# State-space output products of a two-layer trunk: a contiguous tap table, and state products issued over two tiles and two parities at a time

## The chip, the cores and the metric

The kernel runs on one core of one Trainium2 chip. The metric is the device time of one execution in microseconds. An execution is one launch of the whole trunk.

## The reference, cut to what matters

The reference is a trunk of two layers over 1024 frames of 1024 channels in float32. Layer 0 mixes the frames with an RWKV-7 recurrence. Layer 1 mixes them with a diagonal complex state-space layer. Each mixer is followed by a layer norm, a squared-ReLU MLP of width 4096 and another layer norm. The change touches the state-space layer alone. It has 64 groups of 16 channels, and each group drives 64 complex states:

```python
bu_re = jnp.einsum('tbgc,gpc->tbgp', u_c, bbar_re)
bu_im = jnp.einsum('tbgc,gpc->tbgp', u_c, bbar_im)
pr, pi, sr, si = lax.associative_scan(combine, (a_ch_re, a_ch_im, bu_re, bu_im), axis=0)
carry_re, carry_im = cmul(pr, pi, h_re[None], h_im[None])
s_re = sr + carry_re
s_im = si + carry_im
y = (jnp.einsum('tbgp,gcp->tbgc', s_re, cr_w)
     - jnp.einsum('tbgp,gcp->tbgc', s_im, ci_w))
...
y = y.transpose(2, 0, 1, 3, 4).reshape(bsz, seq, d) + xf * d_skip.astype(f32)
y = jax.nn.gelu(y).astype(x.dtype)
z = y @ w_glu
return z[..., :d] * jax.nn.sigmoid(z[..., d:])
```

## The kernel before

The sequence is worked in two halves of 512 frames, and channels lie on partitions in 8 tiles of 128. Large products (projections, MLP, GLU) take each weight block of 128 x 512 from DRAM (`wload`, L169), split it on ACT and DVE into a high and a low part (`whi` L148, `wlo` L149), and do three matmuls for each 128 x 128 piece (L188). `wraw` has two buffers, `whi` and `wlo` three each. One engine, SP, issues nearly all transfers, in order.

The state-space layer doesn't run frame by frame. It cuts a half into 64 chunks of SL = 8 frames, and it needs three tables, which `s5_tables` builds once, tile by tile (f = 0 to 7, four pairs of groups a tile), and keeps in DRAM:

- `tB` carries a chunk's inputs to its state,
- `tC` carries the state at a chunk's start to the chunk's 8 outputs (the state products),
- `tT` carries the inputs of a chunk to its own outputs (the tap products). It is a banded matrix: the row of input frame s is the same list of taps, shifted by s frames. ACT copies the taps out of PSUM (`pk`) into `kpad`, whose front is zero (L1155), and two transfers a tile read `kpad` with overlapping windows and write the shifted rows to `tT` (L1159). `kpad` is `[128, 16, 16, 4]`, so the four groups g lie innermost, next to each other.

`s5` runs once for each half. It turns the input (`u`, `ug`), makes the chunk states (`pbu`, L1206, into `hb`), runs the scan over chunks on DVE and GpSimd (`advance`), and then makes the outputs in four blocks, f2 = 0 to 3, of two tiles each (j = 0, 1). For each tile it loads `tt` from `tT` (L1240) and `tcm` from `tC` (L1242); both share the tag `tab` with four buffers, so one block fills them all. A parity (par = 0, 1) is one of a pair of groups. For each parity there is one PSUM bank `py` (the pool `pc` has two). Into it go the tap products (L1250: 128 rows of the array, 64 columns, tile j in column half j) and then the state products (L1255: 64 rows, the half named by the parity, and 64 columns, the half named by the tile). ACT copies the bank to `y1` (L1257). TensorE turns it back (`pyt`, L1263), DVE adds the skip term, ACT does the GELU, and SP stores `y` (L1268), which the GLU loads later (`yl`, L946).

The order of the work is set by a scheduler. It takes each step's rank (`rank`: lower comes first, where its inputs are there) and a time that it reckons itself. The state-space layer has rank 99300 or 99400, the tables 99500, and the MLP of the other half comes later by its rank, so MLP matmuls stand in every place between the state-space steps.

Of the kernel before, what the change touches and what calls it, by code (L numbers as in the profile page):

```python
# [8 lines left out]
F32 = mybir.dt.float32  # L9
# [9 lines left out]
HT = 512  # L19
KT = 8  # L20
# [12 lines left out]
TB = 2  # L33
LN8R = 400000
# [36 lines left out]
def trunk(ctx, tc, A):  # L71
    nc = tc.nc
    V, S, G, PE, SP = nc.vector, nc.scalar, nc.gpsimd, nc.tensor, nc.sync
# [88 lines left out]
    def wload(src, kt, n, key=None):  # L162
# [19 lines left out]
        return out  # L182

# [836 lines left out]
    SL = 8  # L1020
    NSC = HT // SL
    tT = dr.tile([KT, 128, 2, 512], F32, name="tT")
# [3 lines left out]
    def s5_tables():  # L1026
# [78 lines left out]
        kpad = pp.tile([128, 16, 16, 4], F32, name="kpad")  # L1105
        G.memset(kpad, 0.0)
        for f in range(KT):
# [45 lines left out]
            for par in range(2):  # L1153
                ps_ = slice(64 * par, 64 * par + 16)
                S.copy(kpad[ps_, 8:].rearrange("p t c g -> p g (t c)"), p[ps_])  # L1155
            tv = tT[f].rearrange("(s c) two n -> two c s n", c=16)
            for par in range(2):
                src = kpad[64 * par : 64 * par + 16, 1:9].rearrange("p t c g -> p (t c g)")
                SP.dma_start(tv[par], bass.AP(src.tensor, src.offset, [src.ap[0], (64, SL), src.ap[1]]))  # L1159
# [13 lines left out]
    def s5(H, h):  # L1173
# [61 lines left out]
        for f2 in range(4):  # L1235
            y1 = s5p.tile([128, SL, 4, 2, 16], F32, tag="u1", name="y1", bufs=2)
            tabs = []
            for f in (2 * f2, 2 * f2 + 1):
                tt = s5p.tile([128, 2, 512], F32, tag="tab", name="tt", bufs=4)
                SP.dma_start(tt, tT[f])  # L1240
                tcm = s5p.tile([128, 4, 2, 128], F32, tag="tab", name="tcm", bufs=4)
                SP.dma_start(tcm, tC[f])  # L1242
                tabs.append((f, tt.rearrange("p two (n g) -> p two g n", g=4), tcm))
            for par in range(2):
                qs = slice(64 * par, 64 * par + 64)
                p = pc.tile([128, HT], F32, tag="c", name="py").rearrange("p (g n) -> p g n", g=4)

                for g2 in range(4):
                    for j, (f, tv, tcm) in enumerate(tabs):
                        PE.matmul(p[64 * j : 64 * j + 64, g2], ug[f][:, 2 * g2 + par], tv[:, par, g2],  # L1250
                                  start=g2 == 0, stop=False, skip_group_check=True)
                for g2 in range(4):
                    for ri in range(2):
                        for j, (f, tv, tcm) in enumerate(tabs):
                            PE.matmul(p[64 * j : 64 * j + 64, g2], hb[qs, 4 * f + g2, ri, 0:NSC], tcm[qs, g2, ri],  # L1255
                                      start=False, stop=ri == 1, skip_group_check=True)
                S.copy(y1[:, :, :, par].rearrange("p t g c -> p g t c"), p.rearrange("p g (t c) -> p g t c", t=SL))  # L1257
# [138 lines left out]
```

## Time and profile before

| | us |
|---|---|
| median of three runs (2736.28 to 2744.62) | 2736.43 |
| the profiled execution | 2746.6 |
| its span in the profile | 2744.8 |
| TensorE busy in the span | 2598.4 |
| tap products, 256 records, first and last start | 1401.4 and 2055.1 |
| state products, 512 records, first and last start | 1481.2 and 2057.1 |

The profile is of one execution on the core, with times from the span's start. Each engine's instructions are grouped by source line and tile names, without buffer numbers. An fp32 matmul of the program is two matmul records in the trace. A record's end is modelled, so records of neighbouring matmuls overlap, and a pace is read from the starts.

### The profile page before, as it was taken

How to read it: one execution, taken by the hardware profiler on the slowest of the kernel's cores; microseconds unless marked ns; L12 is line 12 of the kernel's file. 1: busy time of each engine (PE TensorE's matmuls, PEld its weight loads, DVE VectorE, ACT ScalarE, POOL GpSimd, SP SyncE). 2: the span in 40 equal slices, each digit the busy share in tenths (PEclk: the TensorE clock that was granted, in tenths of full speed). 3: DMA queues.
4: the chain of work that ended last, by engine and by line, in shares of the span. 5: the costliest groups of instructions: out<-in, count | busy, mean ns of one | idle time of the engine just before them, and what ended most of it. 6: DMA issues, size and time to landing. Idle time of an engine off the chain costs nothing.

```text
span 2744.8 us, 43807 instructions
## 1 busy us (share of the span) xinstructions
PE 2598.4 (95%) x16582; PEld 2089.9 (76%) x16582; DVE 1813.3 (66%) x3191; ACT 1154.8 (42%) x2038; POOL 630.6 (23%) x515
## 2 busy tenths in 40 slices
PE   7999979989899999989999999999999999999997
PEld 5778757678677777767876788778778887788886
DVE  7477677577786867997567553674855546755556
ACT  7455574544543333353532332434223324433334
POOL 3121542432442122342122000120220101210101
PEclk9989979999899999999999999999999999999998
DMA  4765455564223334545333533233343322333333
GB/s 146 235 214 175 151 164 156 178 203 142 81 86 88 93 92 148 141 129 163 100 112 127 174 95 100 81 96 112 103 164 110 96 96 81 119 96 96 96 96 100
DMA packets 215058, 345.90 MB, mean 126 GB/s; under 512 B 21184, under 2 KB 75584, under 8 KB 214848
## 3 DMA queue, kind: packets, MB, share of 16 engines
q1 hardware_dynamic: 214848, 343.10, 40.5%
q8 instruction: 131, 2.15, 0.3%
q14 instruction: 79, 0.65, 0.1%
HBM read 279.06 MB, written 63.96 MB: 125 GB/s over the span
## 4 chain that ended last, share of the span: by engine, by line
PE 44%; DVE 4%; issue 3%; DMA 1%; POOL 1%; ACT 1%; ACTq 0%; SPq 0%; DVEq 0%; POOLq 0%
PE d L188 39%; PE py L1250 1%; PE py L1255 1%; DVE wlo L149 1%; DMA wraw<-in_mw_dram 1%; PE pu L154 1%; PE pbu L1206 1%; POOL rl L975 1%; DVE hA L991 0%; DMA s_y<-yg 0%; DVE t L1218 0%; DVE hB L991 0%; ACT whi L148 0%; DVE sq L876 0%; PE pu L1195 0%
## 5 line engine op out<-in xcount | busy, mean ns | idle before, releaser
L148 ACT CAST whi<-wraw 128x512 fp32r<-128x512 f32 x668 | 413.5, 620 | 929.1 <-PE d L188 623.2
L149 DVE TENSOR_TENSOR wlo<-wraw,whi 128x512 fp32r<-128x512 f32 x668 | 500.6, 750 | 426.8 <-ACT whi L148 404.3
L188 PE MATMUL d<-qbuf,whi 128*128 128x512 f32 (+1 forms) x2112 | 657.0, 394 | 23.8 <-DVE hA L991 12.8
L188 PEld LDWEIGHTS d<-qbuf,whi 128*128 128x128 f32 x2112 | 391.8, 191 | 120.0 <-DVE hA L991 17.8
L188 PE MATMUL d<-qbuf,wlo 128*128 128x512 f32 (+1 forms) x1056 | 411.9, 392 | 10.7 <-DVE wlo L149 10.4
L975 POOL TENSOR_TENSOR rl<-rl 128x512 f32<-128x512 f32 x128 | 157.2, 1228 | 1094.5 <-ACT rl L974 1094.5
L188 PE MATMUL d<-oAh,whi 128*128 128x512 f32 (+1 forms) x960 | 390.9, 411 | 15.5 <-ACT ev L418 6.3
L188 PE MATMUL d<-oAl,whi 128*128 128x512 f32 (+1 forms) x960 | 387.5, 405 | 3.0 <-DVE oAl L149 2.8
L188 PE MATMUL d<-oAh,wlo 128*128 128x512 f32 (+1 forms) x960 | 386.5, 405 | 2.4 <-DVE wlo L149 2.3
L188 PE MATMUL d<-oBh,whi 128*128 128x512 f32 x704 | 279.2, 397 | 0.0
L188 PE MATMUL d<-oBh,wlo 128*128 128x512 f32 x704 | 278.7, 396 | 0.2 <-DVE wlo L149 0.2
L188 PE MATMUL d<-oBl,whi 128*128 128x512 f32 x704 | 277.1, 394 | 0.0
L188 PEld LDWEIGHTS d<-qbuf,wlo 128*128 128x128 f32 x1056 | 201.7, 191 | 56.5 <-DVE wlo L149 14.5
L188 PEld LDWEIGHTS d<-oAh,whi 128*128 128x128 f32 (+1 forms) x960 | 185.9, 194 | 62.2 <-ACT ev L418 8.4
L188 PEld LDWEIGHTS d<-oAh,wlo 128*128 128x128 f32 (+1 forms) x960 | 185.8, 194 | 44.4 <-DVE wlo L149 3.2
L188 PEld LDWEIGHTS d<-oAl,whi 128*128 128x128 f32 (+1 forms) x960 | 185.6, 194 | 43.1 <-DVE oAl L149 5.2
L991 DVE TENSOR_TENSOR hB<-hB,d 128x512 f32<-128x512 f32 (+1 forms) x256 | 165.0, 650 | 71.2 <-PE d L188 68.0
L991 DVE TENSOR_TENSOR hA<-hA,d 128x512 f32<-128x512 f32 x240 | 162.1, 682 | 64.4 <-PE d L188 62.1
L188 PEld LDWEIGHTS d<-oBh,wlo 128*128 128x128 f32 x704 | 132.9, 189 | 32.4 <-issue 2.0
L188 PEld LDWEIGHTS d<-oBl,whi 128*128 128x128 f32 x704 | 133.1, 189 | 29.9 <-issue 0.7
L188 PEld LDWEIGHTS d<-oBh,whi 128*128 128x128 f32 x704 | 133.1, 189 | 29.0 <-issue 1.2
L149 DVE TENSOR_TENSOR qbuf<-rl,qbuf 128x512 fp32r<-128x512 f32 x128 | 95.0, 742 | 73.5 <-ACT qbuf L148 73.5
(374 smaller groups left out, 3804.8 us busy)
## 6 DMA issues: line engine op xcount, KB each, us to landing
wraw<-in_mw_dram SPq DMA_DIRECT2D x520, 256.0 KB, 2.7
wraw<-in_glu_dram SPq DMA_DIRECT2D x64, 256.0 KB, 2.7
low<-wlo SPq DMA_DIRECT2D x52, 256.0 KB, 2.6
wlo<-low SPq DMA_DIRECT2D x52, 256.0 KB, 3.6
wraw<-in_wk_dram SPq DMA_DIRECT2D x32, 256.0 KB, 3.5
wraw<-in_wr_dram SPq DMA_DIRECT2D x32, 256.0 KB, 3.9
wraw<-in_wv_dram SPq DMA_DIRECT2D x32, 256.0 KB, 4.3
yl<-s_y SPq DMA_DIRECT2D x32, 256.0 KB, 3.1
```

The source lines that it names most:

```text
L148: S.copy(hi, src)
L149: (e or V).tensor_sub(lo, src, hi.bitcast(F32))
L154: PE.matmul(out, x, idt, start=True, stop=True)
L188: bulk.append((PE.matmul(p, w, x, **kw).ins, x.shape[-1]))
L975: G.tensor_mul(r, r, r)
L991: V.tensor_add(z, z, p)
L1206: PE.matmul(p[qs, g2, ri], tb[:, g2, ri, qs], u[:, 2 * g2 + par], start=True, stop=True)
L1250: PE.matmul(p[64 * j : 64 * j + 64, g2], ug[f][:, 2 * g2 + par], tv[:, par, g2], start=g2 == 0, stop=False, skip_group_check=True)
L1255: PE.matmul(p[64 * j : 64 * j + 64, g2], hb[qs, 4 * f + g2, ri, 0:NSC], tcm[qs, g2, ri], start=False, stop=ri == 1, skip_group_check=True)
```

## The change

There are two edits and one helper.

The tap table `tT` becomes one array with the partition first, `[128, 2, KT, 4, 128]`, in which the 128 taps of a group lie next to each other; `kpad` is laid out the same way and holds TBF = 4 tiles. ACT's copies fill it tile by tile. After every fourth tile, 16 transfers (two parities by eight shifts) write four tiles at once, in runs of 512 bytes; before, two transfers a tile wrote runs of 2 KB. The load of a tile takes two runs of 2 KB a partition instead of one of 4 KB, and the tap matmuls read their 128 columns with unit stride instead of a stride of four.

The output block takes both `py` banks at its start, does the tap products of both parities, and then the state products with the loops turned: pair of groups, real and imaginary, tile, parity. `inorder` ties each state product to the one before it by a dependence without a semaphore, so the scheduler keeps them in this order. Both banks are copied out at the end.

```diff
+    def inorder(prods):
+        for x, y in zip(prods, prods[1:]):
+            tc.add_manual_dep(y.ins, x.ins.name, mybir.DependencyInfo(
+                mybir.DependencyClass.NoSync, mybir.DependencyReason.DATA), reason="order")
...
-    tT = dr.tile([KT, 128, 2, 512], F32, name="tT")
+    tT = dr.tile([128, 2, KT, 4, 128], F32, name="tT")
...
-        kpad = pp.tile([128, 16, 16, 4], F32, name="kpad")
+        kpad = pp.tile([128, TBF, 4, 16, 16], F32, name="kpad")
...
-                S.copy(kpad[ps_, 8:].rearrange("p t c g -> p g (t c)"), p[ps_])
-            tv = tT[f].rearrange("(s c) two n -> two c s n", c=16)
-            for par in range(2):
-                src = kpad[64 * par : 64 * par + 16, 1:9].rearrange("p t c g -> p (t c g)")
-                SP.dma_start(tv[par], bass.AP(src.tensor, src.offset, [src.ap[0], (64, SL), src.ap[1]]))
+                S.copy(kpad[ps_, f % TBF, :, 8:].rearrange("p g t c -> p g (t c)"), p[ps_])
+            if f % TBF == TBF - 1:
+                for par in range(2):
+                    for s in range(SL):
+                        SP.dma_start(
+                            tT[16 * s : 16 * s + 16, par, f - TBF + 1 : f + 1].rearrange("c f g n -> c (f g) n"),
+                            kpad[64 * par : 64 * par + 16, :, :, 1 + s : 9 + s].rearrange("c f g t e -> c (f g) (t e)"))
...
-                SP.dma_start(tt, tT[f])
+                SP.dma_start(tt.rearrange("p two (g n) -> p two g n", g=4), tT[:, :, f])
...
-                tabs.append((f, tt.rearrange("p two (n g) -> p two g n", g=4), tcm))
+                tabs.append((f, tt.rearrange("p two (g n) -> p two g n", g=4), tcm))
+            pp = [r.tile([128, HT], F32, tag=t, name="py").rearrange("p (g n) -> p g n", g=4)
+                  for r, t in ((pc, "c"), (pc, "c"))]
+            for g2 in range(4):
+                for par in range(2):
+                    for j, (f, tv, tcm) in enumerate(tabs):
+                        PE.matmul(pp[par][64 * j : 64 * j + 64, g2], ug[f][:, 2 * g2 + par], tv[:, par, g2],
+                                  start=g2 == 0, stop=False, skip_group_check=True)
+            prods = []
+            for g2 in range(4):
+                for ri in range(2):
+                    for j, (f, tv, tcm) in enumerate(tabs):
+                        for par in range(2):
+                            qs = slice(64 * par, 64 * par + 64)
+                            prods.append(PE.matmul(pp[par][64 * j : 64 * j + 64, g2], hb[qs, 4 * f + g2, ri, 0:NSC],
+                                                   tcm[qs, g2, ri], start=False, stop=ri == 1, skip_group_check=True))
+            inorder(prods)
             for par in range(2):
-                qs = slice(64 * par, 64 * par + 64)
-                p = pc.tile([128, HT], F32, tag="c", name="py").rearrange("p (g n) -> p g n", g=4)
-                for g2 in range(4):
-                    for j, (f, tv, tcm) in enumerate(tabs):
-                        PE.matmul(p[64 * j : 64 * j + 64, g2], ug[f][:, 2 * g2 + par], tv[:, par, g2],
-                                  start=g2 == 0, stop=False, skip_group_check=True)
-                for g2 in range(4):
-                    for ri in range(2):
-                        for j, (f, tv, tcm) in enumerate(tabs):
-                            PE.matmul(p[64 * j : 64 * j + 64, g2], hb[qs, 4 * f + g2, ri, 0:NSC], tcm[qs, g2, ri],
-                                      start=False, stop=ri == 1, skip_group_check=True)
-                S.copy(y1[:, :, :, par].rearrange("p t g c -> p g t c"), p.rearrange("p g (t c) -> p g t c", t=SL))
+                S.copy(y1[:, :, :, par].rearrange("p t g c -> p g t c"), pp[par].rearrange("p g (t c) -> p g t c", t=SL))
```

What the scheduler makes of it shows in the order of each engine's instructions (line numbers of the changed kernel are higher by 7 to 15). First TensorE in the first half's third output block, before:

```order
L1250 MATMUL py<-tt,ug 64x128
L1263 MATMUL pyt<-ident,y_13970 128x64 x16
L1250 MATMUL py<-tt,ug 64x128 x7
L1255 MATMUL py<-tcm,hb 64x128
L1250 MATMUL py<-tt,ug 64x128 x5
L1255 MATMUL py<-tcm,hb 64x128 x15
L1250 MATMUL py<-tt,ug 64x128 x3
L1255 MATMUL py<-tcm,hb 64x128 x16
```

and the same block in the changed kernel, with the next MLP matmul (L195) behind it:

```order
L1260 MATMUL py<-tt,ug 64x128
L1278 MATMUL pyt<-ident,y_13986 128x64 x16
L1260 MATMUL py<-tt,ug 64x128 x15
L1268 MATMUL py<-tcm,hb 64x128 x32
L195 MATMUL d<-oBh,wlo 128x512
```

All tap products now stand ahead of all state products; before, the kinds took turns. Inside such a block, with buffer numbers, the place where tap products (from `tt`) give way to state products (from `tcm`) in the second block of the changed kernel; py_13995 and py_13996 are the banks of the two parities, tcm_13989 and tcm_13993 the tables of the two tiles:

```order
L1260 MATMUL py_13995<-tt_13991,ug_13597 64x128
L1260 MATMUL py_13996<-tt_13987,ug_13566 64x128
L1260 MATMUL py_13996<-tt_13991,ug_13597 64x128
L1268 MATMUL py_13995<-tcm_13989,hb_13451 64x128
L1268 MATMUL py_13996<-tcm_13989,hb_13451 64x128
L1268 MATMUL py_13995<-tcm_13993,hb_13451 64x128
L1268 MATMUL py_13996<-tcm_13993,hb_13451 64x128
```

Four state products in a row name the four pairs of tile and parity, and the next four do so again. Before, 16 of one parity stood in a row, with the tile changing from one to the next.

Second, SP while the tables are built, before (two `tT` stores a tile):

```order
L1144 DMA tC<-ca 1024x1x128
L169 DMA wraw<-in_wo_dram 128x512 x2
L1159 DMA tT<-kpad 16x8x512 x2
L169 DMA wraw<-in_wo_dram 128x512
L1110 DMA bc<-in_s5bc_dram 128x256
```

and in the changed kernel around the first row of `tT` stores:

```order
L170 DMA wraw<-in_mw_dram 128x512
L1166 DMA tT<-kpad 16x16x128 x16
L1177 DMA tB<-bs 128x1024
L1151 DMA tC<-ca 1024x1x128
L1117 DMA bc<-in_s5bc_dram 128x256
L170 DMA wraw<-in_mw_dram 128x512 x4
```

The stores stand in two rows of 16 instead of eight pairs, and weight loads wait behind each row.

More of the change, by code (lines that the diff above doesn't have):

```diff
@@ L33 @@
 TB = 2
+TBF = 4
 LN8R = 400000
```

## The prediction

> **What bounds the kernel now.** I read the page first, for the busiest engine:
>
> ```profile
> PE 2598.4 (95%) x16582; PEld 2089.9 (76%) x16582; DVE 1813.3 (66%) x3191; ACT 1154.8 (42%) x2038; POOL 630.6 (23%) x515
> ```
>
> A share over the whole span says little about one stage, so the second view is busy time by stretches (start and end, length, then busy time and instructions of PE, PE's weight loads, DVE, ACT and POOL, the granted clock, DMA's share and GB/s). 1480 to 1535 and 2008 to 2062 are the output products of the two halves of the state-space layer, where the change's matmuls run; 1180 to 1240 is the worst part of the table building.
>
> ```profile
> 1480.00:1535.00 55.00, 55.00 (x503) 41.16 (x502) 22.63 (x30) 18.75 (x31) 8.68 (x5) 0.98 0.63 221
> 2008.00:2062.00 54.00, 54.00 (x489) 40.33 (x489) 22.00 (x29) 17.66 (x31) 9.49 (x6) 0.97 0.56 195
> ...
> 1180.00:1240.00 60.00, 49.40 (x239) 37.46 (x237) 56.91 (x81) 30.89 (x50) 26.36 (x19) 0.86 0.43 113
> ```
>
> In both output stages TensorE is busy all of the time, DVE and ACT under half. What those products take is paid in the end time, since mlp matmuls fill every space between them and would simply come earlier. In the table stage it is the other way: DVE is at 57 of 60 and PE has 10 us of holes.
>
> Third, PE in order of time through three of the four output blocks of the first half (start, length, line, operation, count). Each fp32 matmul of the program stands as two records.
>
> ```profile
> 1381.98 2.09 PE L1206 MATMUL pbu<-ug,tb 128*64 128x64 f32 x64
> ...
> 1401.39 1.07 PE L1250 MATMUL py<-tt,ug 128*64 128x128 f32 x4
> 1407.86 3.84 PE L1250 MATMUL py<-tt,ug 128*64 128x128 f32 x28
> ...
> 1481.22 3.55 PE L1255 MATMUL py<-tcm,hb 64*64 64x128 f32 x64
> ...
> 1489.03 0.65 PE L1250 MATMUL py<-tt,ug 128*64 128x128 f32 x2
> 1489.60 1.01 PE L1263 MATMUL pyt<-ident,y 64*128 64x64 f32 x16
> 1490.55 2.01 PE L1250 MATMUL py<-tt,ug 128*64 128x128 f32 x14
> 1492.49 1.96 PE L1255 MATMUL py<-tcm,hb 64*64 64x128 f32 x32
> 1494.38 2.01 PE L1250 MATMUL py<-tt,ug 128*64 128x128 f32 x16
> 1496.33 1.96 PE L1255 MATMUL py<-tcm,hb 64*64 64x128 f32 x32
> ...
> 1503.26 0.65 PE L1250 MATMUL py<-tt,ug 128*64 128x128 f32 x2
> ...
> 1504.78 2.01 PE L1250 MATMUL py<-tt,ug 128*64 128x128 f32 x14
> 1506.71 0.43 PE L1255 MATMUL py<-tcm,hb 64*64 64x128 f32 x2
> 1507.07 1.56 PE L1250 MATMUL py<-tt,ug 128*64 128x128 f32 x10
> 1508.56 1.96 PE L1255 MATMUL py<-tcm,hb 64*64 64x128 f32 x30
> 1510.45 1.10 PE L1250 MATMUL py<-tt,ug 128*64 128x128 f32 x6
> 1511.48 1.96 PE L1255 MATMUL py<-tcm,hb 64*64 64x128 f32 x32
> ```
>
> A row's length holds its last record's tail, 0.07 of which lies beside the next row (2.01 against 1492.49 - 1490.55 = 1.94). Two paces come out, with the length of one record from this view:
>
> ```profile
> L1255 PE MATMUL py<-tcm,hb x512: 269/269/473, 1481.2 to 2057.2; 64*64 64x128 f32 x171
> L1250 PE MATMUL py<-tt,ug x256: 388/406/422, 1401.4 to 2055.1; 128*64 128x128 f32 x128
> ```
>
> State products (L1255): the two tiles of a block sit in two column halves and start together, so 32 records are 16 starts; (1.96 - 0.27) / 15 = 0.113 us a step. Tap products (L1250): 16 records are 8 starts, (2.01 - 0.41) / 7 = 0.229, for the same 128 columns. The tap table is read with a stride of four elements ("n g" rearranged), the state table is not. Full height isn't the reason: L1206 also uses 128 rows by 64 columns, reads unit stride, and puts 64 records of half the width into 2.09. With 0.22 off for its last record, an estimate from its shorter streaming, that is 0.060 a step, 0.12 for 128 columns.
>
> **The change part by part.** First, the tap products read contiguously. I take 0.113 for the step, as in L1255; the ends are 0.229 (nothing gained, if the layout is not what slows them) and 0.113. By the changed order a block has one tap matmul ahead of the transposes and 15 behind, and the two kinds no longer alternate. Now the lone one takes 0.57 to the next row, and a run of 7 steps 1.94, of which 0.34 is its end. Then the lone one is 0.57 - 2 x 0.116 = 0.35, the other 15 are 15 steps of 0.113 and an end of 0.34 - 0.12 = 0.22, so 1.92: 2.27 a block. The first block of a half (2 matmuls, then 14) gets 0.56 + 1.92. Per half 0.56 + 1.92 + 3 x 2.27 = 9.3. Before, tails taken off: 1.00 + 3.77 in the first block, 0.57 + 1.94 + 1.95 in the second, 0.57 + 1.93 + 1.49 + 1.03 = 5.02 in the third and, by its like order, the fourth: 19.3. Saved 10.0 a half, **20.0 in all** (the second stage is as full and as long).
>
> Second, the state products, four in a row: tile and parity change from one to the next, over two banks, so all four quarters of the array are named in turn. Before, one parity's 16 stood whole before the other's. Whether four quarters run at once, the trace shows in one place: in the first block the parities follow each other without anything between (the x64 row), and there the number of records in flight, in windows of 10 ns, goes up:
>
> ```profile
> 1482.50:1482.51 0.01, 0.01 (x6) 1.00 0.53 205
> 1482.98:1482.99 0.01, 0.01 (x8) 1.00 0.00 0
> 1483.09:1483.10 0.01, 0.01 (x10) 1.00 0.00 0
> 1483.70:1483.71 0.01, 0.01 (x4) 1.00 0.00 0
> ```
>
> A record lasts 0.27, so two a step of 0.11 keep 5 in flight and four keep 10. At the seam it is 10: four quarters at the pair's own step. I take that: 15 x 0.113 + 0.19 (1.89 less 15 steps) = 1.89 a block, and 0.2 more in the first, whose start is slow: 7.8 a half. Before: 3.48 + (1.89 + 1.89) + 2 x (0.36 + 1.89 + 1.89) = 15.5. Saved 7.7 a half, **15.5 in all**; the other end is 0 (pairs only).
>
> The Trainium skill speaks against this: "TensorE: Matmul & The Clock Gate", section "Part 3: Packing small matmuls — row/col tiling", has matmuls start and end strictly in program order. The seam differs: in strict order five records of the first parity and the second's first pair, some seven, could be in flight there, not ten. By the rule the 15.5 would be 0; the measurement decides, and the first rival is worked out below.
>
> Third, what is put at risk in the output stage. Its transfers stay and their time shrinks. SP's issues there, and what moved from 1488 to 1534 with the median time to landing:
>
> ```profile
> 1497.27 0.42 SPq L1268 DMA_DIRECT2D s_y<-yg  x1
> 1498.32 0.32 SPq L1240 DMA_DIRECT2D tt<-tT  x1
> 1498.73 0.46 SPq L1242 DMA_DIRECT2D tcm<-tC  x1
> ...
> DMA packets 4123, 10.86 MB, mean 236 GB/s; under 512 B 458, under 2 KB 458, under 8 KB 4120
> ...
> tt<-tT SPq DMA_DIRECT2D x4, 512.0 KB, 5.1
> ```
>
> The second tile's tables can be asked for only when the block before has let go of their buffers (1496.33 + 1.89 = 1498.22, and tt goes out at 1498.32), and SP, in order, also holds a store and a load of y ahead of them. Should those make tt 1.0 late, it lands 6.1 behind the state products; the next block's second tile wants it after the mlp matmuls (1498.22 to 1503.26, 5.0), one tap (0.35) and the transposes (1490.55 - 1489.60 = 0.95), 6.3 behind. It just fits, and any delay on SP becomes a wait of the tap matmuls, with all of PE behind them. A block to block time of 14.2 (1489.03 to 1503.26) becomes 10, and the 10.86 MB of 46 us have to pass in about 32, 340 GB/s. I charge 5 us in all (six seams of just under 1 us), from 0 to 14.
>
> Fourth, the tables. Rows of the building:
>
> ```profile
> L1155 ACT COPY kpad<-pk x16: 1055/1074/1087, 1126.9 to 1267.7; 16x512 f32<-16x512 f32 x16
> L1159 SPq DMA_DIRECT2D tT<-kpad x16: 320/362/1264, 1128.6 to 1268.9; - x16
> 1072.42 0.96 POOL L1106 MEMSET kpad<- 128x1024 f32 x1 [0.91 <-POOL rl L975]
> 1075.99 1.11 POOL L975 TENSOR_TENSOR rl<-rl 128x512 f32<-128x512 f32 x1 [2.61 <-ACT rl L974]
> ACT whi L148 <- DMA wraw<-in_mw_dram: 23.0, 12, 3.9
> ```
>
> The memset, four times as long at 3.9 us, ends 0.3 after POOL's next square could start: nothing. The 16 copies on ACT write contiguously and may halve (0.5 us each, on an engine at half load): nothing. Eight pairs of stores become two rows of sixteen, 16 x 0.36 = 5.8 us each on SP, with a table store and the weight loads behind them; ACT already waits 23 us there for late weights. Against that, six of eight places where SP stands still for a copy go. The next copy into the same slot comes about 20 us later (eight pairs in 141 us) and the row is through in 5.8 + 5, so that wait hides. I charge 1 us, from -5 to +8.
>
> Sum: -20.0 - 15.5 + 5 + 1 = -29.5 on the profiled 2746.6, 2717.1. That execution stands 0.37% over the median of 2736.43, so 2717.1 x 0.9963 = 2707.
>
> **The rivals.** A: PE starts matmuls only in order. The two records of a matmul need the same quarter, so each matmul's second record holds the next matmul back: eight records take four steps, the pair's rate. The taps alone, with less haste in the transfers: -20.0 + 2 + 1 = -17, 2719. For it: the only four-wide stretch is a few steps long, and no run of any length here issues four quarters. It is the page's rule above. B: transfers set the pace of the output stage. If it gets no more than the 269 GB/s of one 20 us stretch there, 10.86 MB take 40 us instead of 32: 16 in place of the 5, -18.5, 2718; at today's 236 GB/s -6.5, 2730. Rows for B and for C:
>
> ```profile
> 1500.00:1520.00 20.00, 10.03 (x100) 6.56 (x102) 0.00 (x0) 1.17 (x2) 1.00 0.74 269
> ...
> 545.01 1.71 PE L596 MATMUL pA<-AR,KB 64*128 64x128 f32 x16
> ```
>
> DMA is at 0.74 there, so full use would be about 360, above what is needed. C, slower: changing the row half at each matmul empties the array. A lone state matmul (the x2 row) takes 0.36 to the next row; at that price the 256 of them take 92 us instead of 31: -20 + 61 + 3 = +44, 2780. It decides from (31 + 20) / 256 = 0.20 us a matmul. Against it: pA changes row halves at each matmul, and (1.71 - 0.27) / 15 = 0.096 a record shows no emptying (no overlap either, which leans to A, though its weights are twice as wide).
>
> **How the numbers follow.** Forecast 0.68, A 0.13, B 0.12, C 0.03, unforeseen stalls from the reordering 0.04. The range runs from 35.5 saved with 5 gained in the tables (-40.5, 2696) up to 2722, past A and B's nearer end; B's far end, C and both costs at their worst stay out. A measurement here tells 0.3%, 8.2 us. Faster: the forecast, A and most of B, 0.90; same 0.05; slower 0.05.
>
> **What would show it.** Tap steps of 0.11 instead of 0.23; 64 state records in about 1.9 with ten in flight; PE full from block to block. Wrong: tap steps still near 0.23 (layout no cause); state runs of 3.5 (A); PE waiting ahead of tap matmuls for tt (B); holes of several us behind the rows of sixteen stores.

## The result, and the profile after

The changed kernel takes 2754.73 us (median of four runs, 2754.32 to 2756.34), against 2738.43 for the kernel before on the same chip (four runs, 2736.28 to 2744.62). The ratio is 1.0057, with a 95% interval from 1.0044 to 1.0070: slower by 15.6 us, where 29.5 less were forecast. The profiled execution took 2754.32, its span 2752.5. Since the profiled execution of before was one of its longer ones, the two spans differ by 7.7 only. The engines over the span:

```profile
PE 2572.3 (93%) x16582; PEld 2078.3 (76%) x16582; DVE 1814.6 (66%) x3191; ACT 1145.8 (42%) x2038; POOL 631.8 (23%) x515
```

TensorE is busy 26.1 us less than before (2598.4), but the part of the span in which it stands still went from 146.4 (2744.8 - 2598.4) to 180.2. The products did get cheaper. TensorE in the changed kernel's second block of outputs, in order of time (start, length, line, count):

```profile
1508.21 1.01 PE L1278 MATMUL pyt<-ident,y 64*128 64x64 f32 x16
1509.16 1.96 PE L1260 MATMUL py<-tt,ug 128*64 128x128 f32 x30
1511.05 1.98 PE L1268 MATMUL py<-tcm,hb 64*64 64x128 f32 x64
```

Here 30 records of tap products stand for 15 matmuls. They take 1.89 (1511.05 - 1509.16), 0.126 a step with the run's end in it, where a step took 0.229 before. The 64 state records take 1.91 to the next row (1512.96), 30 ns a record. So both products run as forecast where nothing disturbs them. Where the time went shows in TensorE's busy time by stretches (stretch, length, busy time, granted clock, DMA's share, GB/s), first before:

```profile
1100.00:1350.00 250.00, 230.97 (x1253) 0.96 0.49 136
...
1470.00:1550.00 80.00, 76.13 (x583) 0.96 0.56 191
...
1990.00:2080.00 90.00, 85.84 (x625) 0.96 0.45 153
```

and then the changed kernel:

```profile
1100.00:1350.00 250.00, 213.25 (x1081) 0.90 0.46 125
...
1470.00:1550.00 80.00, 68.43 (x599) 0.91 0.55 177
...
1990.00:2080.00 90.00, 76.54 (x632) 0.92 0.46 148
```

In the table stage (1100 to 1350) and in the two output stages TensorE lost 17.7, 7.7 and 9.3 us of busy time, and in each the granted clock of what was left is lower by 0.04 to 0.06. In each stretch between these (0 to 1100, 1350 to 1470, 1550 to 1990, 2080 to 2700) the two kernels differ by 1.4 us of busy time or less.

In the table stage, SP shows why:

```profile
1167.12 0.33 SPq L170 DMA_DIRECT2D wraw<-in_mw_dram  x1
1167.49 19.48 SPq L1166 DMA_DIRECT2D tT<-kpad  x16
...
1191.15 1.80 SPq L170 DMA_DIRECT2D wraw<-in_mw_dram  x2
```

The row of sixteen stores holds SP for 19.48 us, 1.2 a store and not 0.36, and the next weights are asked for 24 us after the last. The second row does the same:

```profile
1271.41 19.16 SPq L1166 DMA_DIRECT2D tT<-kpad  x16
1290.67 1.12 SPq L1177 DMA_DIRECT2D tB<-bs  x1
1291.88 2.49 SPq L170 DMA_DIRECT2D wraw<-in_mw_dram  x2
```

The waits between 1165 and 1300 (engine, line, releaser: us in total, times, longest) carry it on to TensorE:

```profile
ACT whi L149 <- DMA wraw<-in_mw_dram: 31.7, 5, 20.4
...
PE d L195 <- ACT whi L149: 16.1, 2, 13.5
...
ACT kpad L1162 <- DMA tB<-bs: 7.1, 1, 7.1
PE pb L1175 <- ACT kpad L1162: 6.9, 1, 6.9
```

The waits of 20.4 and 13.5 belong to the second row. Before, ACT's longest wait for weights was 3.9. Behind the first row TensorE stood still twice, for 6.9 us and, from 1193.62, for another 2.6, until a copy of weights that ACT began at 1195.54. The 6.9 come from `kpad` itself: ACT's next copy into it waits for all stores of the row, and it starts at 1191.87, when the last of them has landed (1191.70; the view names `tB`, whose store lands later, at 1192.94). Without that wait TensorE would still have lacked weights until 1196.2, so both holes together, some 9.5 us, are what the late weights alone would have cost there. In the output stage, SP's order stands in front of the second tile's tables:

```profile
1526.25 0.33 SPq L1283 DMA_DIRECT2D s_y<-yg  x1
1526.67 0.52 SPq L1249 DMA_DIRECT2D tt<-tT  x1
1527.29 1.51 SPq L1251 DMA_DIRECT2D tcm<-tC  x1
1529.88 0.32 SPq L953 DMA_DIRECT2D yl<-s_y  x1
1531.94 0.32 SPq L1283 DMA_DIRECT2D s_y<-yg  x1
1532.36 0.52 SPq L1249 DMA_DIRECT2D tt<-tT  x1
```

The first tile's tt is asked for at 1526.67, the second's at 1532.36, behind a load of y that waits for its store and a store that waits for its GELU. TensorE wants the second at 1534 and gets it at 1538.36 (in brackets the wait ahead of the row):

```profile
1521.60 3.51 PE L1260 MATMUL py<-tt,ug 128*64 128x128 f32 x30 [2.01 <-DMA tt<-tT]
...
1538.36 3.67 PE L1260 MATMUL py<-tt,ug 128*64 128x128 f32 x30 [4.42 <-DMA tt<-tT]
```

The same 30 records that took 1.96 above now take 3.51 and 3.67. The stretches of these two rows say why; the granted clock is the number behind the brackets:

```profile
1521.60:1525.00 3.40, 3.40 (x30) 3.11 (x30) 1.84 (x3) 1.66 (x3) 0.87 (x1) 0.53 0.55 152
...
1538.40:1542.00 3.60, 3.60 (x34) 3.27 (x34) 2.09 (x3) 1.15 (x2) 0.00 (x0) 0.50 0.34 123
```

So these waits of 2.0 and 4.4 us cost their own length and some 1.7 us more, because the clock stands at half for the next 3.5 us. Not every such wait does that: in the third and eighteenth run below, waits of 2.20 and 2.42 us ahead of the same records left the clock at 1.00 and the records at 1.96.

### The profile page after: what moved, and what is told of

The parts are those of the page before. It is cut to its first block, busy times and chain, and to the rows that moved or that the text cites. A ratio compares the mean times of both kernels' runs of the same rounds, so it can differ in the third digit from the quotient of the medians.

```text
span 2752.5 us, 43811 instructions
## 1 busy us (share of the span) xinstructions
PE 2572.3 (93%) x16582; PEld 2078.3 (76%) x16582; DVE 1814.6 (66%) x3191; ACT 1145.8 (42%) x2038; POOL 631.8 (23%) x515
## 4 chain that ended last, share of the span: by engine, by line
PE 58%; DVE 15%; DMA 5%; issue 4%; ACT 3%; SPq 2%; POOL 1%; ACTq 0%; DVEq 0%; POOLq 0%
PE d L195 51%; DVE wlo L150 3%; SPq L1166 1%; DMA yl<-s_y 1%; DMA s_y<-yg 1%; PE pA L603 1%; DVE hA L998 1%; DMA wraw<-in_mw_dram 1%; DMA ldsg<-s_sg 1%; PE pu L155 1%; PE pbu L1215 1%; DVE t L1227 1%; DVE hB L998 1%; DVE xh L648 1%; DVE x L646 1%
## 5 line engine op out<-in xcount | busy, mean ns | idle before, releaser
L195 PE MATMUL d<-qbuf,whi 128*128 128x512 f32 (+1 forms) x2112 | 659.3, 395 | 40.0 <-DVE hA L998 14.2
L195 PEld LDWEIGHTS d<-qbuf,whi 128*128 128x128 f32 x2112 | 393.7, 192 | 136.2 <-DVE hA L998 20.6
L195 PE MATMUL d<-qbuf,wlo 128*128 128x512 f32 (+1 forms) x1056 | 412.8, 393 | 9.2 <-DVE wlo L150 8.8
L195 PE MATMUL d<-oAh,whi 128*128 128x512 f32 (+1 forms) x960 | 390.0, 410 | 16.3 <-ACT ev L425 5.2
L195 PE MATMUL d<-oAl,whi 128*128 128x512 f32 (+1 forms) x960 | 386.8, 404 | 2.5 <-DVE oAl L150 2.2
L195 PE MATMUL d<-oAh,wlo 128*128 128x512 f32 (+1 forms) x960 | 385.9, 405 | 2.5 <-DVE wlo L150 2.0
L195 PE MATMUL d<-oBh,whi 128*128 128x512 f32 x704 | 278.5, 396 | 0.7 <-ACT whi L149 0.7
L195 PE MATMUL d<-oBh,wlo 128*128 128x512 f32 x704 | 278.1, 395 | 0.0
L195 PE MATMUL d<-oBl,whi 128*128 128x512 f32 x704 | 277.5, 394 | 0.0
L195 PEld LDWEIGHTS d<-qbuf,wlo 128*128 128x128 f32 x1056 | 201.9, 191 | 56.2 <-DVE wlo L150 14.1
L195 PEld LDWEIGHTS d<-oAh,whi 128*128 128x128 f32 (+1 forms) x960 | 185.2, 194 | 61.3 <-ACT ev L425 7.3
L195 PEld LDWEIGHTS d<-oAh,wlo 128*128 128x128 f32 (+1 forms) x960 | 185.3, 193 | 44.8 <-DVE wlo L150 3.4
L195 PEld LDWEIGHTS d<-oAl,whi 128*128 128x128 f32 (+1 forms) x960 | 185.4, 193 | 42.6 <-DVE oAl L150 4.7
L195 PEld LDWEIGHTS d<-oBh,wlo 128*128 128x128 f32 x704 | 132.8, 189 | 32.2 <-issue 2.0
L195 PEld LDWEIGHTS d<-oBl,whi 128*128 128x128 f32 x704 | 132.8, 189 | 30.2 <-issue 1.3
L195 PEld LDWEIGHTS d<-oBh,whi 128*128 128x128 f32 x704 | 133.0, 189 | 29.0 <-ACT whi L149 1.3
```

The lines of the kernel that those rows point to most:

```text
L195: bulk.append((PE.matmul(p, w, x, **kw).ins, x.shape[-1]))
```

## The experiments

Each kernel ran beside the kernel before on the same chip; ratios are to that kernel, with 95% intervals. A difference between two ratios is turned into us with 2738; with intervals of some 0.001 to 0.002 to either side, such a difference is good to 5 to 8 us. "Output stages" below means, for each half, from the first state product to the last transpose: 52.7 us twice before, with TensorE busy throughout, 50.5 and 46.6 in the changed kernel with 42.4 and 40.2 busy. Some 496 records of TensorE run in it in every kernel, or 502 in the first half of those with the long rows of stores.

### Which of the two parts

**First run**: the kernel before, with the changed output block (both banks, products four in a row) and the old table.

```diff
 kernel before
+            prods.append(PE.matmul(pp[par][...], hb[...], tcm[qs, g2, ri], ...))
+            inorder(prods)
```

> The old table (strided, two stores a tile) with the new order of the state products alone. Theory T: both products got cheaper as forecast (some 35 us), and holes on TensorE with a lower granted clock behind them took it back, some 25 us in the table stage (two rows of sixteen stores) and some 25 in the two output stages (waits for tt). Here the table stage is that of before, so T expects no holes there, state products at 1.9 us a block, -15.5 from these, and some of it lost at the seams, since a block still keeps its long taps (4 us): 0 to 8. So 7 to 15 us less than before. Rival R1 (the rows of stores are the whole loss): -15 to -16. Rival R2 (the output stage loses whatever is gained there, since its transfers set the pace): 0, within 3 us of before. Rival R3 (the four-in-a-row order itself costs time outside, by the clock): slower than before.

Measured: 0.9997 [0.9981, 1.0013], about 1 us less. The 31.2 us of state products before (from each start to the next, waits taken out, over all 512 records) became 15.3. The stages shrank to 46.0 and 46.6, so 12.8 us are there to be seen, but TensorE waits 2.7 and 3.2 in them. T's 7 to 15 isn't met, nor R1's 15 to 16, and R2's number is. Where the rest of the 12.8 went this run doesn't say; the fourteenth comes back to it.

**Second run**: the changed kernel with the old output block.

```diff
 changed kernel
-            inorder(prods)
+            for par in range(2): ... taps, then states of one parity
```

> The contiguous table with its two rows of sixteen stores, and the state products in the old order, one parity after the other. T: tap products -20, table stage +25, seams of the output stage 5 to 12: between 10 and 17 us slower than before, so about the changed kernel's time or a little more (the state products bring nothing, and less is lost at the seams). R1: +5 (-20 + 25). R2: +25, since the taps bring nothing and the table stage loses what it lost. R3: faster than before, by some 10 to 20 us.

Measured: 1.0059 [1.0039, 1.0080], 16 us slower. The tap products went from 38.6 to 21.4, and the table stage lost as much as in the changed kernel (77.9 of 100 busy from 1200 to 1300, at a clock of 0.84). That is T's case; the numbers of R1, R2 and R3 aren't met.

### The table stage

**Third run**: the contiguous table, stored tile by tile.

```diff
-    tT = dr.tile([128, 2, KT, 4, 128], F32, name="tT")
+    tT = dr.tile([KT, 128, 2, 4, 128], F32, name="tT")
...
-            if f % TBF == TBF - 1:
-                ... 16 stores of [16, 16, 128], four tiles at once
+            for par in range(2):
+                for g in range(4):
+                    SP.dma_start(tv[par, :, :, g], ...)   # [16, 8, 128], one tile
```

> The changed kernel, but the table is stored tile by tile, eight stores of 64 KB a tile (a parity and a pair of groups each, runs of 512 bytes as before), instead of two rows of sixteen of 128 KB. The same bytes, twice the stores, no row in front of the weight loads longer than eight. T: the two holes of the table stage (13.5 and 6.9 us, and the clock behind them) shrink to a third or less: 15 to 25 us less than the changed kernel, 0 to 10 less than before. R1: 25 to 50 us less than the changed kernel, since all loss was there. If the number of 512-byte packets costs, however they are dealt out, the 64 stores take SP as long in all, and the gain is under 8 us. R3: no change against the changed kernel.

Measured: 0.9975 [0.9961, 0.9988], 7 us less than before and 22 less than the changed kernel. TensorE in the table stage:

```profile
1100.00:1350.00 250.00, 228.78 (x1269) 0.98 0.48 136
```

That is near before (230.97) again, with the same packets of 512 bytes and twice the stores. The output stages are much as in the changed kernel (48.7 and 48.5, with 39.3 and 40.9 busy). So the bunching of the stores costs, not the layout of the taps, and some 23 us of the forecast are still missing. The order of the tiles in DRAM changes with this edit too; the fifteenth run below keeps the changed kernel's and shows the same.

**Eighth run**: the long rows, issued by GpSimd.

```diff
-                        SP.dma_start(tT[16 * s : 16 * s + 16, ...], kpad[...])
+                        G.dma_start(tT[16 * s : 16 * s + 16, ...], kpad[...])
```

> The changed kernel with its two rows of sixteen stores of the table, but issued by GpSimd in place of SP. The packets and bytes are the same, in the same two bursts. If the holes of 6.9 and 13.5 us come from SP, which stands 19 us in a row and can't issue the weight loads behind it (T): the holes go, and 15 to 25 us less than the changed kernel. If they come from the DMA engines, busy with 2048 packets of 512 bytes a burst, so that weights would be late whoever issues (R4): the holes stay at half their size or more, and under 10 us gained.

Measured: 1.0072 [1.0059, 1.0085], nothing gained. (A row is 4096 packets of 512 bytes, 2.1 MB, not the 2048 of the expectation.) SP is free now and asks for the weights, but they are late all the same. The DMA issues from 1172 to 1216 (count, KB each, median us from issue to landing):

```profile
tT<-kpad POOLq DMA_DIRECT2D x16, 128.0 KB, 9.7
wraw<-in_mw_dram SPq DMA_DIRECT2D x7, 256.0 KB, 8.7
```

and the same weights among the pairs of stores of before (1125 to 1190):

```profile
wraw<-in_mw_dram SPq DMA_DIRECT2D x6, 256.0 KB, 3.0
```

So R4 holds in this form: the burst fills the DMA engines, and SP's queue only shows it. GpSimd's queue cut the stores into packets of other sizes and held up GpSimd's own work, so how much of the loss comes from which isn't told apart here. The rate of such a burst can be read from both kernels, before (one pair, 0.5 MB):

```profile
1128.60:1133.60 5.00, 5.00 (x26) 4.13 (x25) 4.81 (x6) 2.29 (x5) 3.56 (x3) 1.00 0.79 148
```

and after (one row, 2.1 MB):

```profile
1167.50:1190.00 22.50, 16.08 (x91) 11.07 (x90) 18.62 (x29) 4.25 (x8) 6.10 (x4) 1.00 0.75 111
```

At a DMA share of 0.75 to 0.79 these stores out of 16 partitions move 111 to 148 GB/s; in an output stage a share of 0.72 moves 247 (fourteenth run, quoted below). The bytes take the engines about as long in eight pairs as in two rows: eight times under 5 us, hidden behind the weights in hand, or twice 19.

**Fifteenth run**: rows of half the size.

```diff
-TBF = 4
+TBF = 2
```

> The changed kernel with TBF = 2: four rows of sixteen stores, each store 64 KB, in place of two rows with 128 KB. The same bytes and packets, the same layout. A row holds 1 MB, which at the 110 GB/s of the long rows takes the DMA engines some 9 us instead of 19. Theory T on the table stage (the weights in hand cover some 7 to 10 us; what a burst lasts longer is a hole): the holes of 6.9 and 13.5 us shrink to 0 to 3 each, and 12 to 22 us less than the changed kernel. If a hole's size goes with the bytes stored and not with the burst's length: no change.

Measured: 1.0010 [0.9998, 1.0022], 13 us less than the changed kernel. The first and the last of the four rows on SP:

```profile
1142.31 9.42 SPq L1166 DMA_DIRECT2D tT<-kpad  x16
...
1263.84 9.68 SPq L1166 DMA_DIRECT2D tT<-kpad  x16
```

With a row's length the time goes: eights that hold SP about 4 us 0.9975, rows of 9.6 us 1.0010, rows of 19.3 us 1.0057. The holes are smaller (3.4, 2.7, 3.3 and 2.0 us, and one of 4.2 ahead of a pk), but not gone. A row of 9.6 leaves a hole of some 3. One of 19.2 left 13.5, and one of 19.5 left 9.5 (6.9 and 2.6). So the weights in hand cover some 6 to 10 us, near the 7 to 10 that I had put into T.

### The output stages: a wait that is handed on

**Fourth run**: yg in slots that are free by then.

```diff
-                y = s5p.tile([128, HT], F32, tag="yg", name="yg", bufs=1)
+                y = s5p.tile([128, HT], F32, tag="ug", name="yg", bufs=8)
```

> The changed kernel, but yg (the result that is stored to y) takes the slots of ug that the block's taps have set free, instead of one buffer of its own, so DVE and ACT no longer wait for a store to land before they turn to the next tile. The transfers stay, with both stores of a block ahead of the second tile's tables. If the single buffer is what makes tt late (theory T1 on the seams): the waits for tt shrink to a third, and 10 to 20 us less than the changed kernel. If tt is late because SP asks for it only when a block's last state product has read the buffers, and the table then takes 5 to 6 us to land (T2): under 5 us less, and the waits for tt stay. R1: no change, since the seams cost nothing.

Measured: 1.0064 [1.0044, 1.0084], no gain. The waits ahead of the taps stayed (1.9 and 2.9 in the first half, 4.6 and 0.8 in the second). T1 falls.

**Fifth run**: the third run's kernel, y stored by ACT.

```diff
-                SP.dma_start(scr["y"][...], y)
+                S.dma_start(scr["y"][...], y)
```

> The kernel of the third run (four-in-a-row products, contiguous table stored in eights) with one more edit: ACT issues the stores of y, behind its own GELU, in place of SP, so the loads of the next tables on SP no longer stand behind a store that waits for DVE and ACT. Theory T3 (SP's order: the second tile's tt is asked for some 4 us after its buffer is free, because the store ahead of it waits for its GELU): the waits for tt, some 13 us in two stages, go to under 4, and 8 to 20 us less than the third run's kernel, so 14 to 26 less than before. Rival B (the transfers set the pace; DMA's share in the stage is 0.73 over 42 us): the waits stay, moved by a microsecond or two, and under 4 us gained. Rival T2 (the buffers come free too late, after the last state product, and a table needs 5 us): the waits shrink by a quarter at most, under 5 us.

Measured: 1.0030 [1.0017, 1.0043], 15 us slower than the third run, against every theory's number. SP's waits in the first output stage (1470 to 1560), in the third run:

```profile
SPq L1283 <- ACT yg L1282: 16.5, 7, 6.5
SPq L953 <- DMA s_y<-yg: 14.0, 8, 3.7
```

and in the fifth:

```profile
SPq L953 <- DMA s_y<-yg: 40.1, 8, 8.2
```

The wait for the GELU left SP, but what SP has next, the load of y, waits for the same store to land, and with a single yg these loads go out 7 to 10 us apart. The tables still stand behind it. T3 named the right queue and the wrong instruction.

**Sixth run**: the fifth with yg in the slots of ug (the fourth run's edit). **Seventh run**: the sixth with a block's loads as tt, tt, tcm, tcm.

```diff
+                SP.dma_start(tt, ...)    # both tiles first
+                SP.dma_start(tcm, ...)
```

> The kernel of the fifth run, and yg in the slots of ug that the taps have set free (as in the fourth run). T3: the stores no longer stand in front of the tables, so the single buffer could only delay DVE and ACT; with it gone too, 0 to 6 us less than the fifth run. If the single buffer was what held the blocks back all the time, only masked in the fourth run by SP's order: 8 to 15 us less than the fifth run. B: no change.

> The kernel of the sixth run, with the loads of a block in the order tt, tt, tcm, tcm in place of tt, tcm, tt, tcm, so both tap tables take the buffers that the taps set free, some 2 us ahead of those that the state products set free. T2: 5 to 12 us less than the sixth run. T3 or B: within 4 us of it.

Measured: 0.9981 [0.9969, 0.9993] and 0.9982 [0.9971, 0.9993]. The sixth is 13 us below the fifth, as the theory of a masked buffer had it, and no better than the third. The seventh gains nothing: its waits for tt are gone, and waits for tcm stand in their place (5.2 and 4.5 us in the two stages). So T2's number isn't met; but SP still stood with the loads of y, so this run alone doesn't exclude T2. The thirteenth does: its buffers come free no sooner, and the waits are nearly gone. SP in the sixth run (1470 to 1560):

```profile
SPq L953 <- DMA s_y<-yg: 16.3, 5, 6.3
```

**Ninth run**: the sixth with the loads of y by GpSimd. **Tenth run**: the ninth with the taps of one parity alone loaded (and used for both). **Twelfth run**: the same edits on y, with the old table.

```diff
-            SP.dma_start(y, scr["y"][k * 128 : ...])
+            G.dma_start(y, scr["y"][k * 128 : ...])
...
-                SP.dma_start(tt, ...)                      # tenth run
+                SP.dma_start(tt[:, 0], tT[f, :, 0] ...)
```

> The kernel of the sixth run, with the loads of y for the GLU (yl) issued by GpSimd. SP now issues only tables and weights in the output stage; in the sixth run it stood 16.3 and 14.7 us in the two stages with a yl that waited for its store to land, the next tt behind it. T3 (SP's order is what makes tt late): waits ahead of tap products from 6 to 8 us a stage to under 2, and 10 to 20 us less than the sixth run, so 15 to 25 us less than before. T2 or B (buffers come free too late for a load of 5 us, or the transfers set the pace): 0 to 5 us less than the sixth run, and the waits stay at 5 us or more a stage.

> The kernel of the ninth run, but only the taps of one parity are loaded, and both parities' products use them: a quarter of the tables' bytes is left out, and the output isn't the reference's. TensorE's instructions are the same. T3: nothing more to gain, within 4 us of the ninth run. B (bytes set the pace): 8 to 15 us less than the ninth run. T2: a tt of half the size lands 1.5 to 2 us sooner, 5 to 10 us less.

> The first run's kernel (old table, four-in-a-row state products) with the three edits on queues and buffers. In the first run the state products' 15.7 us came out as about nothing. T3: the seams of the first run (4.5 and 1.4 us more idle time, and the clock behind them) go, and 8 to 16 us less than before appear. T2 or B: within 4 us of the first run.

Measured: 1.0017 [1.0004, 1.0030], 1.0024 [1.0013, 1.0036] and 1.0026 [1.0014, 1.0037]. The ninth is 10 us slower than the sixth and the twelfth 8 slower than the first, where no theory had a loss. With a quarter of the tables' bytes gone the tenth run isn't faster than the ninth, so bytes don't set the pace there, which speaks against B. In the ninth, what TensorE waited for in and behind the first stage (1466 to 1530):

```profile
PE d L195 <- DVE hB L998: 6.3, 2, 5.3
PE py L1260 <- DMA tt<-tT: 3.8, 3, 2.8
PE pyt L1278 <- ACT y L1272: 3.3, 1, 3.3
```

The waits for tt have shrunk from 13 us in the two stages to 4.5, and two new ones stand beside them. The twelfth shows them without the first: its first stage took 43.3 us with TensorE busy all the time, and then came a hole of 7.4 and, in the second half, one of 8.5. Waits in the first stage there:

```profile
POOL yl L952 <- DMA s_y<-yg: 38.2, 4, 17.7
...
PE d L194 <- DVE hB L997: 8.5, 2, 7.4
```

The second row is the end of a chain. TensorE waits for a bank that DVE's add (L997, at 1529.19) sets free; DVE stood 7.7 us with the split of y ahead of it, that waited for ACT's half of the split, ACT 7.9 for the load, and the load on GpSimd 17.7 for its store. The 8.5 of the second half is a copy of py on ACT, behind a split of y that waited for its load. The wait had moved to whichever in-order queue held y.

**Thirteenth run**: the sixth, with the loads of y on SP, tied behind the half's last store of y. **Fourteenth run**: the same with the old table.

```diff
+                lasty[H] = S.dma_start(scr["y"][f * 128 : ...], y)
...
+            yd = SP.dma_start(y, scr["y"][k * 128 : ...])
+            if H in lasty:
+                inorder([lasty[H], yd])
```

> The kernel of the sixth run (products and table as changed, table stored in eights, y stored by ACT, yg in the slots of ug), with the eight loads of y for the GLU back on SP and tied behind the half's last store of y, so that none stands among the tables. In the ninth run GpSimd stood 38 to 42 us a stage with such a load in front of the squares of the MLP, and ACT waited for y in front of the copies of py; holes of 3.3, 5.3 and 8.8 us came from that, while the waits for tt had gone from 13 to 4.5. Theory T4 (each in-order engine that holds a transfer of y in the stage hands its wait to TensorE; the products' 30 us appear only when none does): idle of the two output stages from 17 to under 6 us, no new hole of over 3 us behind them, and 15 to 28 us less than before. Rival B (transfers set the pace): waits for tt of 6 us a stage or more, and within 5 us of the sixth run. Rival R5 (the stage is short of other work: with the products shorter, the weights' copies on ACT and DVE don't keep up and the hole only moves behind the stage): idle behind the stage, at the next MLP matmuls, of 5 us or more, and within 5 us of the sixth run.

> The twelfth run's kernel (old table, four-in-a-row state products, y stored by ACT, yg in the slots of ug) with the loads of y on SP behind the half's last store. The twelfth run had a first stage of 43.3 us without a hole, and then lost 7.4 and 9.2 us to y on GpSimd and ACT. T4: both stages of 43 to 44 us, and 10 to 17 us less than before. R5: 0 to 5 us less than before.

Measured: 0.9912 [0.9895, 0.9928], 24 us less than before, and 0.9942 [0.9923, 0.9961], 16 less. The two stages of the thirteenth run (PE busy, then its weight loads, DVE, ACT, POOL):

```profile
1471.30:1511.70 40.40, 38.75 (x496) 32.10 (x495) 17.62 (x23) 15.44 (x26) 8.08 (x5) 0.96 0.74 254
1990.10:2028.20 38.10, 36.97 (x496) 30.54 (x495) 17.37 (x22) 14.13 (x25) 8.05 (x5) 1.00 0.70 236
```

and the first of the fourteenth:

```profile
1475.60:1518.80 43.20, 43.20 (x496) 32.71 (x495) 17.75 (x23) 15.44 (x26) 7.95 (x5) 1.00 0.72 247
```

The thirteenth run's kernel beats both the kernel before and the changed one. Its stages are 12 to 15 us shorter than before and nearly full, those of the fourteenth run 9.5 and full. They move 208 to 254 GB/s, where those of the first six runs, which waited, moved 192 to 240, so B falls. No hole of over 1.6 us stands behind the thirteenth run's stages (R5 falls). The third block of the thirteenth run, with the longest wait that is left in its stages:

```profile
1488.43 1.01 PE L1282 MATMUL pyt<-ident,y 64*128 64x64 f32 x16
1490.96 3.62 PE L1264 MATMUL py<-tt,ug 128*64 128x128 f32 x30 [1.52 <-DMA tt<-tT]
1494.51 1.98 PE L1272 MATMUL py<-tcm,hb 64*64 64x128 f32 x64
```

**Eleventh and sixteenth run**: controls, the kernel before with the edits on y of the ninth and of the thirteenth run, and nothing else.

> The kernel before with the three edits on queues and buffers alone (stores of y by ACT, loads of y by GpSimd, yg in the slots of ug). Its TensorE never waited in the output stages (0.0 us). All theories: within 4 us of before. If it is faster by 8 us or more, the edits help somewhere else, and the ninth run's gain isn't that of the products.

> The control: the kernel before with the three edits on y alone (stored by ACT, yg in the slots of ug, loads of y behind the half's last store). TensorE had no hole in its output stages, so T4 gives nothing: within 4 us of before. If it is faster by over 8 us, part of the thirteenth run's 25 us is not the products'.

Measured: 0.9997 [0.9982, 1.0012] and 1.0002 [0.9990, 1.0014]. The edits on y do nothing for the kernel before, so the thirteenth run's gain is that of the products.

**Seventeenth run**: the changed kernel whole, with the edits on y. **Eighteenth run**: the third run's kernel with the loads of y behind the last store alone; stores of y stay on SP, yg keeps its one buffer.

> The changed kernel whole, with its two rows of sixteen stores, and the three edits on y. If the two losses are independent (table stage and output stages each cost what their own holes and the clock behind them take), it stands over the thirteenth run by what the rows cost, 20 to 26 us: 2733 to 2739, so 16 to 23 less than the changed kernel and within 5 us of before. If the rows cost only because the output stages behind them are short too, it comes within 10 us of the thirteenth run.

> The third run's kernel with one edit: the loads of y behind the half's last store. SP keeps the stores of y and yg its one buffer. In the third run SP waited 14.0 and 13.3 us for y to land ahead of a load, and 16.5 and 16.5 us for a GELU ahead of a store. T4: only the first part goes; holes of 4 to 8 us a stage stay, and the time lies between the third and the thirteenth run, 6 to 16 us less than the third. If the loads were the whole of it: within 4 us of the thirteenth run.

Measured: 0.9985 [0.9969, 1.0001] and 0.9934 [0.9915, 0.9953]. The seventeenth's stages are 39.6 and 40.2, as in the thirteenth; it stands 20 us over it, which is the rows. Rows cost 22 without the edits on y and 20 with them, and the queues 20 with rows and 17 without: two losses that add up. The eighteenth lies between the third and the thirteenth, 11 us below the one and, within the noise, 6 above the other, as expected; 2.5 to 3.9 us of waits a stage are left in it, fewer than the 4 to 8 expected.

## Why the prediction was wrong

**The products: right.** State products: 15.5 forecast, 15.7 measured (31.2 to 15.5). Tap products: 20.0 forecast; 18.6 in the thirteenth run (38.6 to 20.0), 13.8 in the changed kernel (24.8), where the taps behind a wait ran at half the clock. Four quarters of the array do run at once, so rival A falls. It was worked out from two things: the rule of the Trainium skill ("TensorE: Matmul & The Clock Gate", "Part 3: Packing small matmuls — row/col tiling") that starts and ends stay strictly in program order, and my own assumption that a matmul's second record holds the next matmul back. At four records a step the two can't both hold for this program. The rows don't name a record's quarter, so which of the two fails isn't shown by the changed kernel's pace. Rival C's price appears nowhere.

**The tables: the step that failed first.** The prediction has: "Eight pairs of stores become two rows of sixteen, 16 x 0.36 = 5.8 us each on SP", charged at 1 us with 8 as the far end. A row took 19.5, and the rows cost 20 to 22 us. 0.36 was the price of an issue with little ahead of it in the queue: the row's first three stores took 0.43 to 0.50 too, the others 0.9 to 1.7. The price of the transfer was in the same trace: the two stores of a pair landed 4.7 us after their issue (median of 16), and a row carries the bytes of four pairs, 18.8. I took the row to be "through in 5.8 + 5" and so hid the next copy's wait behind 20 us of work, and the weights' wait in a charge of 1 us. The first row was through 24.2 us after its start (1167.49 to 1191.70), the copy was ready after 17, and the weights in hand cover some 6 to 10.

**The output stage: the step that failed second.** "It just fits, and any delay on SP becomes a wait", charged at 5 us with 14 as the far end; it cost 17 to 20. Two things were wrong in its price. I put the store and the load of y ahead of tt at the time of their issues, "1.0 late". They are instructions that wait, and the profile of before says how long SP stood with them in its first output stage (1470 to 1560):

```profile
SPq L946 <- DMA s_y<-yg: 16.1, 8, 4.0
SPq L1268 <- ACT yg L1267: 8.6, 4, 3.0
```

That was 25 us in four blocks, free while a block took 14.2 us. With 10 forecast for a block, each of these waits reaches the tables. And I priced a wait at its length. Here it often costs the length and the half clock behind it.

**Rival B** had the sign (tap products that wait for tt) and not the cause: the tenth run took out a quarter of the bytes and gained nothing, and the thirteenth moves its tables at 236 to 254 GB/s without waits to speak of. **The sum**: once both are taken away, 24 us are there of the 35.5 that the products alone were to save. TensorE stands still for 10.0 us more than before (156.4 us of the span against 146.4), about what is missing, though the profile of before is of a longer execution. Where these holes come from is not fully explained: the thirteenth run's tap tables gain 8 us over the fourteenth's old ones, though its tap products are 15.6 shorter (35.6 to 20.0). TensorE stands still for 7.6 us more than there (2710.3 - 2553.9 = 156.4, against 2720.5 - 2571.7 = 148.8); 2.6 of them are the waits for tt, the others are spread over the table stage and the stretches around the output stages, and weren't tried one by one.

## What to carry to other kernels

When work on the busiest engine is made shorter, list every instruction that stands in an in-order queue ahead of its next operands, and read how long that queue waits now while nobody notices: that wait becomes the new bound, and moving it to another engine's queue only moves the hole, until it stands behind everything that is needed sooner. Price a row of transfers by its bytes at the rate that its pattern shows, not by the time of an issue, and ask what the buffers downstream can cover in one piece: the same bytes were hidden here in small lots and cost 20 us in two large ones.

## What the runs showed of the hardware that I had not expected

- Behind a wait of TensorE of 1.5 us (thirteenth run) or 2.0 us (changed kernel) the clock stood at half for the next 3.4 us or so: 30 tap records took 3.5 to 3.7 instead of 1.96. Behind waits of 2.20 us (third run) and 2.42 us (eighteenth) it stayed at 1.00, so the length of the wait alone doesn't decide. The stretches at half clock in the changed kernel between 1100 and 2100 last 3.41, 6.83, 13.65 or 17.07 us, all multiples of 3.41. The Trainium skill ("TensorE: Matmul & The Clock Gate", "Part 1: The HAM clock gate (the "warmup" mystery)") has the half clock after an idle window of about 3.4 us; the half agrees with these rows, the waits that can bring it on are shorter here.
- In the changed kernel, packets of 512 bytes out of 16 partitions took 62 ns each (median of the 4277 of that size from 1167 to 1190, most of them the row's), while those of a store of tC just before, out of 128 partitions, took 27.
- 64 matmul records of 64 x 128, issued over the four quarters of the array, pass in 1.91 us, at twice the pace of the same records over two.
